# Recurrence: three block levels in one TensorE visit, differences of inputs and r0 on VectorE

## The chip, the cores and the metric

The kernel runs on one core of a Trainium2 chip. The metric is the device time of one execution in microseconds. The median of three runs before the change is 2112.96 us (2112.58 to 2113.19).

## The reference

A trunk of two decoder layers on 1024 tokens of width 1024, all in float32. Layer 0 mixes tokens with a gated linear recurrence (8 heads of 128), layer 1 with sliding-window attention; each is followed by a gated FFN of width 2816 with a causal convolution of width 3. Only the recurrence is touched here:

```python
def hgrn2_chunkwise(q, k, v, log_f):
    """S_t = diag(f_t) S_{t-1} + k_t v_t^T ; o_t = S_t^T q_t, evaluated chunk by chunk."""
    ...
def hgrn2_mixer(h, w_in, lower_bound, g_norm_w, w_out):
    q, f, i, g = jnp.split(h @ w_in, 4, axis=-1)
    fg = lb + (1.0 - lb) * jax.nn.sigmoid(heads(f))
    o = hgrn2_chunkwise(jax.nn.silu(heads(q)), 1.0 - fg, heads(i), jnp.log(fg))
    o = o * lax.rsqrt(jnp.mean(jnp.square(o), -1, keepdims=True) + RMS_EPS)
    o = o * g_norm_w.astype(jnp.float32) * jax.nn.silu(heads(g))
    return o.reshape(B, S, D).astype(h.dtype) @ w_out
```

## The kernel before, in words

**Number form.** Large products run in fp32r. Each operand is split into a high part and a low part; a product is three matmuls (`mm3`, L200 to L202: high-high, high-low, low-high). ScalarE casts the high part, VectorE subtracts it from the source to give the low part (`low_part`, L175).

**First stage (the first 47 us).** The input `x` comes in eight blocks of 128 tokens. `turn_keep` turns a block on TensorE (L210), ScalarE copies it twice (L959 the high part into `T`, L960 the exact values into `XS`), VectorE makes the low part (L175). `ig_block` multiplies a block with the first head's `i` and `g` weights: per `kc` one matmul of the high part with both weight parts (L846, 512 columns) and one of the low part with the high weights (L847, 256 columns). `lower_bounds` (L1004 to L1018) computes the gates' lower bounds with small instructions on VectorE and an exponential on ScalarE (L1013). Meanwhile GpSimd makes differences of quarters of `x` in place (`sums_of`, L902, 12 of them, 512 columns each) for the fast products that follow; `split_sum` splits them into high (ScalarE, L912) and low (VectorE, L913) parts in `HL` and in `T`, and L924 makes one more sum.

**Second stage.** The products of `f` and `q` of head 0 (96 matmuls), then 14 units (`q`+`f`, or `i`+`g`, of heads 1 to 7). A unit is seven products of half size after Strassen and Winograd (`product(u, p)`, 12 matmuls each), whose weight sums are made by VectorE (L1359, L1595) and split into `WR` (L1350 high, L175 low).

**Recurrence.** `recur` works one head in seven levels: at level i, blocks of 2^i tokens are joined in pairs. `update(i)` (L1171, L1173, L1176 on VectorE) multiplies the decays of a pair into `qp` and `kp`. The scores of level i take `qp` and `kp` as they stand before `update(i)`; where TensorE comes later, `stash(i)` keeps a copy of what the update will overwrite (two copies on ScalarE). Within 32 tokens the scores go to `Ab` (`scores`), above that to `A` (`blocks`): both use matmuls on 32 of the array's columns (`tile_position`), the one at output partition o on column group o/32. TensorE comes to a head in six visits, each squeezed between the 512-column matmuls of the units: (A) levels 8 and 4, column sums of `r0`, `r1`, `r2`; (B) levels 32 and 16; (C) eight transposes of `kp` and level 64; then the products of `kd` with `V`, of `A` with `V` and of `qp` with the state `St`. `r0 = qs * kp` is made by GpSimd (L1182), `r1` by VectorE (L1187).

**What sets the order.** In this part of the program the order on each engine is the order in which the code is laid out. The object `od` (class `Order`) keeps three clocks with estimated costs: `t` for TensorE, `v` for VectorE, `a` for ScalarE. Chains are generators that yield how long they want to wait on TensorE's clock; `od.tick()` after each matmul resumes those that are due. VectorE's small jobs (low parts "lo", weight sums "sum", parts of `x` "x") wait in the list `jobs` and are laid by `lay` when VectorE's clock leaves room, by `need` when a product asks for them, by `breathe` between a head's steps when they are pressing. Before the change, a loop (`while not prepared`) lays the whole preparation of the first unit ahead of the first head's recurrence.

Of the kernel before, what the change touches and what calls it, by code (L numbers as in the profile page):

```python
# [113 lines left out]
def trunk(ctx: ExitStack, tc: tile.TileContext, a: dict, out: bass.AP):  # L114
# [594 lines left out]
    with tc.tile_pool(name="t", bufs=1, reuse_waits="tile") as raws, hgrn_pool as hp:  # L709
# [34 lines left out]
        def group(key):  # L744
            return key[1] if key and key[0] in ("sum", "lo") else key[0] if key else None
# [9 lines left out]
        def first_ready(due=lambda key: True):  # L755
            seen = set()
# [19 lines left out]
        def pressing(key):  # L776
            if not key or key[0] not in ("sum", "lo"):
                return False
            if key[0] == "lo" and key[2] == 4:
                return True  # L780
            p = key[2] if key[0] == "lo" else {1: 5, 2: 6, 3: 7, 4: 4}[key[2]]
            return place_of[key[1], p] <= now[0] + (2 if key[0] == "lo" else 3)
# [54 lines left out]
        def ig_block(us, tp, ahead=None):  # L837
# [4 lines left out]
            for tb in () if ahead else (2 * tp, 2 * tp + 1):  # L842
                ps, ts = psmm(), slice(tb * P, (tb + 1) * P)
                for kc in range(KC):
                    w = us[kc // 4]
                    nc.tensor.matmul(ps, T[:, 0, kc, ts], w[:, :, kc % 4, :], start=kc == 0, stop=False)  # L846
                    nc.tensor.matmul(ps[:, :256], T[:, 1, kc, ts], w[:, 0, kc % 4, :], start=False, stop=kc == KC - 1)  # L847
                    od.t += 0.347
# [50 lines left out]
        def sums_of(t, eng):  # L899
            a11, a12, a21, a22 = [quarter(b, i) for b in (t, t + 4) for i in range(2)]  # L900
            for dst, x0, x1 in ((a11, a21, a11), (a21, a22, a21), (a22, a11, a22)):
                eng.tensor_tensor(dst, x0, x1, op=sub)  # L902
# [13 lines left out]
        def build_sums(go, summed):  # L916
            for t in range(4):
                while t not in summed:
                    yield 0.2
                for which in (7, 6):  # L920
                    split_sum(t, which)
                    yield 0.6
                a12, a22 = quarter(t, 1), quarter(t + 4, 1)
                job(od.t, 0.69, lambda a12=a12, a22=a22: nc.vector.scalar_tensor_tensor(  # L924
                    a12, a22, -1.0, a12, op0=ALU.mult, op1=sub), ("rows", t))
            left = {5: [0, 1, 2, 3], 3: [0, 1, 2, 3]}
            while left[5] or left[3]:
                which = 5 if left[5] and (go or not left[3]) else 3
                while which == 5 and not go:
                    yield 0.2  # L930
                t = left[which].pop(0)
                while which == 3 and ("rows", t) not in done_jobs:
                    yield 0.2
                split_sum(t, which)
                yield 0.6

        with tc.tile_pool(name="ep", bufs=1, reuse_waits="tile") as ep:
# [15 lines left out]
            def turn_keep(tb):  # L953
# [7 lines left out]
                low_part(T[:, 1, :, ts], by_k(XS[:, tb, :]), T[:, 0, :, ts], None)  # L961
# [13 lines left out]
            if True:  # L975
# [28 lines left out]
                def lower_bounds():  # L1004
# [6 lines left out]
                    for r in range(2):  # L1011
                        nc.vector.tensor_tensor(le[:, r, :], par[:, 8 * r:8 * r + 8], lm, op=ALU.subtract)
                    nc.scalar.activation(le, le, AF.Exp)  # L1013
# [19 lines left out]
                def first_split(g, names):  # L1033
                    w0[g] = [hp.tile([P, S], F32R, name=n).rearrange("p (k c) -> p k c", k=KC) for n in names]
                    hi, lo, raw = w0[g][0], w0[g][1], raws0[g].rearrange("p (k c) -> p k c", k=KC)
                    nc.scalar.copy(hi, raw)
                    low_part(lo, raw, hi, None)

                od.fill = lay
                go, summed = [], []  # L1040
                for t in range(2):
                    sums_of(t, nc.gpsimd)
                firsts = [od.spawn(build_sums(go, summed))]
                for tp, after in ((2, 2), (1, 6)):
# [4 lines left out]
                    if after == 2:  # L1049
                        summed.extend((0, 1))  # L1050
                for t in range(2, 4):
                    sums_of(t, nc.gpsimd)
# [5 lines left out]
                summed.extend((2, 3))  # L1058
# [1083 lines left out]
```

## Time and profile before

| | |
|---|---|
| median of three runs | 2112.96 us |
| the profiled execution | 2110.27 us |
| its span, first to last instruction | 2108.5 us |
| mean granted TensorE clock | 0.998 |
| busy: TensorE / VectorE / ScalarE / GpSimd | 2087.6 / 1803.3 / 972.5 / 317.3 us |
| first stage, to the first product of `f` | 0 to 46.76 us |
| units and recurrence | to about 470 us |

How to read it: PE is TensorE's matmuls, PEld its weight loads, DVE VectorE, ACT ScalarE, POOL GpSimd. A matmul in fp32 leaves two records in the trace, so 16 such matmuls show as x32; the start of one record to the start of the next tells the pace, since the durations overlap. `<-` in brackets names what ended the engine's idle time. "L847" is line 847 of the kernel printed above.

### The profile page before, as it was taken

How to read it: one execution, taken by the hardware profiler on the slowest of the kernel's cores; microseconds unless marked ns; L12 is line 12 of the kernel's file. 1: busy time of each engine (PE TensorE's matmuls, PEld its weight loads, DVE VectorE, ACT ScalarE, POOL GpSimd, SP SyncE). 2: the span in 40 equal slices, each digit the busy share in tenths (PEclk: the TensorE clock that was granted, in tenths of full speed). 3: DMA queues.
4: the chain of work that ended last, by engine and by line, in shares of the span. 5: the costliest groups of instructions: out<-in, count | busy, mean ns of one | idle time of the engine just before them, and what ended most of it. 6: DMA issues, size and time to landing. Idle time of an engine off the chain costs nothing.

```text
span 2108.5 us, 31814 instructions
## 1 busy us (share of the span) xinstructions
PE 2087.6 (99%) x12305; PEld 1741.4 (83%) x12305; DVE 1803.3 (86%) x2434; ACT 972.5 (46%) x1576; POOL 317.3 (15%) x323
## 2 busy tenths in 40 slices
PE   8999999999999999999999999999999999999998
PEld 7788888888888888888888888888888888888887
DVE  6978887779999998987977668979999999978986
ACT  5655555542444444444433367733544344444430
POOL 5011111201021122100001123312121122000002
PEclk9999999999999999999999999999999999999999
DMA  4111111324245577638754511052355577559662
GB/s 157 36 46 51 53 51 55 98 85 169 86 149 181 170 158 166 145 113 302 250 190 160 150 36 46 14 169 82 99 166 177 158 169 160 130 158 329 220 213 93
DMA packets 241303, 286.82 MB, mean 136 GB/s; under 512 B 30136, under 2 KB 160112, under 8 KB 241152
## 3 DMA queue, kind: packets, MB, share of 16 engines
q1 hardware_dynamic: 221600, 235.11, 34.6%
q0 software_dynamic: 19264, 49.54, 10.9%
q8 instruction: 97, 1.59, 0.3%
q14 instruction: 54, 0.44, 0.1%
q10 hardware_dynamic: 288, 0.14, 0.0%
HBM read 241.72 MB, written 89.15 MB: 157 GB/s over the span
## 4 chain that ended last, share of the span: by engine, by line
PE 94%; DVE 4%; issue 1%; ACT 1%; DMA 0%; SPq 0%; DVEq 0%; ACTq 0%
PE psmm L200 18%; PE psmm L202 18%; PE psmm L201 18%; PE psax L200 10%; PE psax L201 10%; PE psax L202 10%; PE psax L206 4%; PE psmm L206 1%; PE psmm L210 1%; PE psax L1916 1%; PE psax L210 1%; PE psmm L1743 1%; DVE T L175 0%; DVE r L1187 0%; DVE Y L261 0%
## 5 line engine op out<-in xcount | busy, mean ns | idle before, releaser
L507 DVE SCALAR_TENSOR_TENSOR Y<-Y,cwt 128x1023 f32<-128x1023 f32 (+1 forms) x176 | 225.0, 1281 | 46.1 <-ACT Y L505 44.7
L227 ACT CAST HL<-rx 128x1024 fp32r<-128x1024 f32 (+1 forms) x151 | 151.0, 1006 | 166.2 <-DMA rx<-in_ffn_w_in_dram 39.6
L200 PE MATMUL psmm<-T,HL 128*128 128x512 f32 x512 | 200.6, 392 | 0.0
L202 PE MATMUL psmm<-T,HL 128*128 128x512 f32 x512 | 199.3, 389 | 0.0
L201 PE MATMUL psmm<-T,HL 128*128 128x512 f32 x512 | 199.3, 389 | 0.0
L175 DVE TENSOR_TENSOR HL<-rx,HL 128x1024 fp32r<-128x1024 f32 (+1 forms) x151 | 176.4, 1175 | 17.9 <-ACT HL L227 17.6
L249 POOL TENSOR_TENSOR rs<-rs,nhalf 128x1 f32<-128x1 f32 x32 | 45.3, 1416 | 716.7 <-DVE rs L248 716.7
L505 ACT ACTIVATE Y<-Y,cwt 128x1024 f32<-128x1024 f32 x88 | 108.9, 1238 | 84.7 <-DVE Y L494 79.8
L200 PE MATMUL psax<-T,HL 128*128 128x512 f32 x352 | 137.3, 390 | 0.0
L202 PE MATMUL psax<-T,HL 128*128 128x512 f32 x352 | 137.0, 389 | 0.0
L201 PE MATMUL psax<-T,HL 128*128 128x512 f32 x352 | 136.9, 389 | 0.0
L549 POOL COPY warm<-Y 128x1 f32<-128x1 f32 x64 | 63.4, 990 | 356.3 <-DVE Y L488 349.3
L202 PEld LDWEIGHTS psmm<-T,HL 128*128 128x128 f32 x512 | 96.1, 188 | 20.1
L201 PEld LDWEIGHTS psmm<-T,HL 128*128 128x128 f32 x512 | 96.2, 188 | 19.5
L200 PEld LDWEIGHTS psmm<-T,HL 128*128 128x128 f32 x512 | 96.1, 188 | 19.6
L227 ACT CAST HT<-rx 128x1024 fp32r<-128x1024 f32 (+1 forms) x37 | 35.6, 962 | 133.5 <-DVE rx L462 66.7
L200 PE MATMUL psmm<-T,WR 128*128 128x512 f32 x224 | 90.3, 403 | 0.5 <-DVE GT L1464 0.5
L202 PE MATMUL psmm<-T,WR 128*128 128x512 f32 x224 | 87.4, 390 | 0.0
L201 PE MATMUL psmm<-T,WR 128*128 128x512 f32 x224 | 87.3, 390 | 0.0
L227 ACT CAST HL<-Y 128x1024 fp32r<-128x1024 f32 (+1 forms) x32 | 28.6, 893 | 118.2 <-DVE Y L462 41.2
L202 PEld LDWEIGHTS psax<-T,HL 128*128 128x128 f32 x352 | 66.1, 188 | 13.8
L200 PEld LDWEIGHTS psax<-T,HL 128*128 128x128 f32 x352 | 66.1, 188 | 13.6
(444 smaller groups left out, 6017.1 us busy)
## 6 DMA issues: line engine op xcount, KB each, us to landing
rx<-in_ffn_w_in_dram SPq DMA_DIRECT2D x136, 256.0 KB, 3.8
rx<-gd SPq DMA_DIRECT2D x118, 256.0 KB, 3.7
bsd<-in_ffn_w_out_dram POOLq DMA_DIRECT2D x36, 768.0 KB, 7.2
gd<-Y SPq DMA_DIRECT2D x44, 512.0 KB, 2.6
raw<-in_hgrn_w_in_dram SPq DMA_DIRECT2D x30, 512.0 KB, 5.1
rx<-in_ffn_w_out_dram SPq DMA_DIRECT2D x54, 256.0 KB, 4.5
R<-bsd SPq DMA_DIRECT2D x44, 256.0 KB, 5.1
Y<-in_ffn_w_in_dram SPq DMA_DIRECT2D x40, 256.0 KB, 3.8
```

The costliest lines, as they stand in the source:

```text
L175: make = lambda e: e.tensor_tensor(lo, src, hi.bitcast(F32), op=ALU.subtract)
L200: nc.tensor.matmul(ps, st(0), mv(0), start=start, stop=False, skip_group_check=more)
L201: nc.tensor.matmul(ps, st(0), mv(1), start=False, stop=False, skip_group_check=more)
L202: nc.tensor.matmul(ps, st(1), mv(0), start=False, stop=stop, skip_group_check=more)
L206: nc.tensor.matmul(ps, lhsT, rhs, start=start, stop=stop, **kw)
L210: nc.tensor.transpose(ps, src, ident)
L227: nc.scalar.copy(hi, src)
L249: nc.gpsimd.tensor_tensor(rs, rs, nhalf, op=ALU.pow)
L505: nc.scalar.activation(c, u, AF.Identity, bias=cwt[:, l, 3, ci:ci + 1], scale=cwt[:, l, 2, ci:ci + 1])
L507: nc.vector.scalar_tensor_tensor(c[:, sh:], u[:, :S - sh], cwt[:, l, 2 - sh, ci:ci + 1], c[:, sh:], op0=ALU.mult, op1=ALU.add)
L549: with tc.issue_after(nc.gpsimd.tensor_copy(tick, Y[:, 2 * (fc % 2) + (p == 4), :1]).ins):
L1743: nc.tensor.matmul(ps, T[:, x, kc, tb * P:(tb + 1) * P], us[kc][:, w, :], start=start and kc == 0, stop=False)
```

## The change

1. **Blocks of x.** In `ig_block` the eight matmuls with the high part come first, then the eight with the low part. The low part becomes a job that is laid at the latest between the two (`need(("T", tb))`). In `lower_bounds`, 2.6 us of the planner's time lie ahead of the exponential.
2. **Differences.** The 12 differences of quarters move from GpSimd to VectorE, as jobs "xs"; `build_sums` becomes one chain for each pair of blocks.
3. **First unit.** The loop that laid its preparation in one piece is gone; it is laid beside the first products and the first head.
4. **Planner.** Among the jobs that are ready, the one with the earliest `deadline` is laid, the place of the product that needs it.
5. **r0** moves from GpSimd to VectorE.
6. **Levels 16, 32 and 64.** They go in one visit (B) after `update(5)`: level 64 straight from `kp` and `qp`, level 32 from a `stash(5)` that replaces `stash(6)`. Level 64 is cut into 32 matmuls of 32 columns on four column groups, where there were 16 of 64 columns on two. The transposes of `kp` stay as visit (C). Level 64 is copied to `A` in two pieces.

```diff
@@ planner
+        def deadline(key):
+            if not key or key[0] not in ("sum", "lo") or key[0] == "lo" and key[2] == 4:
+                return -2 if key and key[0] == "T" else -1
+            return place_of[key[1], key[2] if key[0] == "lo" else {1: 5, 2: 6, 3: 7, 4: 4}[key[2]]]
@@ first_ready
                 if ready <= max(od.t, od.v) and due(key):
-                    return i
+                    found.append((deadline(key), i))
+            return min(found)[1] if found else None
@@ ig_block
                 for kc in range(KC):
-                    w = us[kc // 4]
-                    nc.tensor.matmul(ps, T[:, 0, kc, ts], w[:, :, kc % 4, :], start=kc == 0, stop=False)
-                    nc.tensor.matmul(ps[:, :256], T[:, 1, kc, ts], w[:, 0, kc % 4, :], start=False, stop=kc == KC - 1)
-                    od.t += 0.347
+                    nc.tensor.matmul(ps, T[:, 0, kc, ts], us[kc // 4][:, :, kc % 4, :], start=kc == 0, stop=False)
+                    od.t += 0.23
+                    od.tick()
+                if ("T", tb) in pending:
+                    need(("T", tb))
+                for kc in range(KC):
+                    nc.tensor.matmul(ps[:, :256], T[:, 1, kc, ts], us[kc // 4][:, 0, kc % 4, :], start=False, stop=kc == KC - 1)
+                    od.t += 0.117
                     od.tick()
@@ sums_of
-        def sums_of(t, eng):
+        def sums_of(t):
             a11, a12, a21, a22 = [quarter(b, i) for b in (t, t + 4) for i in range(2)]
-            for dst, x0, x1 in ((a11, a21, a11), (a21, a22, a21), (a22, a11, a22)):
-                eng.tensor_tensor(dst, x0, x1, op=sub)
+            for n, (dst, x0, x1) in enumerate(((a11, a21, a11), (a21, a22, a21), (a22, a11, a22))):
+                job(kept[t + 4], 0.61, lambda dst=dst, x0=x0, x1=x1: tt(dst, x0, x1, op=sub), ("xs", t, n))
@@ turn_keep
-                low_part(T[:, 1, :, ts], by_k(XS[:, tb, :]), T[:, 0, :, ts], None)
+                kept[tb] = od.act(2.05)
+                job(od.a, 1.23, lambda: low_part(T[:, 1, :, ts], by_k(XS[:, tb, :]), T[:, 0, :, ts], None), ("T", tb))
+                pending.add(("T", tb))
@@ lower_bounds
+                    yield 2.6
                     nc.scalar.activation(le, le, AF.Exp)
@@ blocks
                 m = 1 << i
+                if m == 2 * BL:
+                    for c in range(NB):
+                        for u in range(2):
+                            for b in range(2):
+                                o, t = m * u + BL * b, c * P + m + BL * u
+                                mm32(pv[o:o + BL, c, m:m + BL], K[:, c * P + BL * b:c * P + BL * (b + 1)], Q[:, t:t + BL],
+                                     cost=0.015, tile_position=(0, o))
+
+                    def put():
+                        for u in range(2):
+                            nc.scalar.copy(A[:m, :, m + BL * u:m + BL * (u + 1)], pv[m * u:m * (u + 1), :, m:m + BL])
+                            od.act(0.4)
+                    return put
@@ recur
-            nc.gpsimd.tensor_tensor(r0, qs, kp, op=ALU.mult)
+            nc.vector.tensor_tensor(r0, qs, kp, op=ALU.mult)
...
+                if j == 0:
+                    next_early = stash(5, hp.tile([P, S], F32, name="St"))
+            yield max(od.a - od.t - 0.2, 0.0)
+            yield from update(5)
+            yield od.behind(0.6, 0.5)
             pv = chunks(psax())
-            high, low = blocks(5, pv, kp, qp), scores(4, pv[:, :, :16], early, early)
-            yield from update(5)
+            last_put = blocks(6, pv, kp, qp)
+            high, low = blocks(5, pv, next_early, next_early), scores(4, pv[:, :, :16], early, early)
+            yield from update(6)
             low()
-            yield od.behind(-0.6, 0.0)
-            early = stash(6, hp.tile([P, S], F32, name="kd"))
-            yield max(od.a - od.t - 0.2, 0.0)
-            yield from update(6)
-            wait = od.behind(0.6, 2.1)
             high()
+            last_put()
...
-            put = blocks(6, chunks(psax()), early, early)
             kd = hp.tile([P, S], F32, name="kd")
             nc.scalar.copy(kd, ps)
-            put()
@@ product
-            if (u, p) in prep:
-                drive(lambda: prep[u, p][1] is None)
+            drive(lambda: (u, p) in casted)
@@ before the units
-            while not prepared:
-                for t in firsts:
-                    if t[1] is not None:
-                        od.step(t)
-                if jobs:
-                    lay_job()
             task = od.spawn(all_heads())
```

Three places in the orders that come out. TensorE at the first full block of `x` (block 4), where `psmm` is the block's accumulator and `psax` takes the transposes of the blocks to come. Before, and then after:

```order
L877 MATMUL psmm<-HL,T 128x256 x8
L846 MATMUL psmm<-HL,T 128x512
L847 MATMUL psmm<-HL,T 128x256
L846 MATMUL psmm<-HL,T 128x512
L847 MATMUL psmm<-HL,T 128x256
```

```order
L884 MATMUL psmm<-HL,T 128x256 x8
L848 MATMUL psmm<-HL,T 128x512 x8
L854 MATMUL psmm<-HL,T 128x256 x3
L210 MATMUL psax<-ident,XS 128x128 x8
L854 MATMUL psmm<-HL,T 128x256 x5
```

The alternation of high and low is gone; the transposes of blocks 2 and 6 now stand among the low passes.

VectorE at the same place: `par`, `lm`, `le`, `lbt` belong to the lower bounds, `T<-XS` is the low part of a block (first block 4, then block 5). Before, and then after:

```order
L175 TENSOR_TENSOR T<-XS,T 128x8x128
L1008 COPY par<-psmm 128x17
L1009 TENSOR_SCALAR par<-par 128x1
L1010 TENSOR_TENSOR lm<-par 128x8
L1012 TENSOR_TENSOR le<-par,lm 128x8 x2
L1015 TENSOR_TENSOR lm<-le 128x8
L1016 RECIPROCAL lm<-lm 128x8
L1017 TENSOR_TENSOR lbt<-le,lm 128x8
L1018 TENSOR_SCALAR lbt<-lbt 128x8
L175 TENSOR_TENSOR T<-XS,T 128x8x128
```

```order
L1023 TENSOR_TENSOR le<-par,lm 128x8 x2
L1027 TENSOR_TENSOR lm<-le 128x8
L1028 RECIPROCAL lm<-lm 128x8
L1029 TENSOR_TENSOR lbt<-le,lm 128x8
L1030 TENSOR_SCALAR lbt<-lbt 128x8
L175 TENSOR_TENSOR T<-XS,T 128x8x128
L909 TENSOR_TENSOR XS<-XS 128x512
L175 TENSOR_TENSOR T<-XS,T 128x8x128
```

The low part of block 4 now stands behind the lower bounds, and the differences (L909) stand among the low parts.

TensorE at the third visit (C) of head 0, between matmuls of the units, where `ident,kp` are the transposes and `psax<-kd` is level 64. Before, and then after:

```order
L201 MATMUL psmm<-T,WR 128x512
L202 MATMUL psmm<-T,WR 128x512
L210 MATMUL psax<-ident,kp 128x128 x8
L206 MATMUL psax<-kd 32x64 x16
L200 MATMUL psmm<-T,WR 128x512
```

```order
L201 MATMUL psmm<-HL,WR 128x512
L202 MATMUL psmm<-HL,WR 128x512
L210 MATMUL psax<-ident,kp 128x128 x8
L200 MATMUL psmm<-HL,WR 128x512
L201 MATMUL psmm<-HL,WR 128x512
```

Level 64 has left this visit; it stands in the one before (B) as 32 matmuls of 32x32 ahead of the other two levels.

More of the change, by code (lines that the diff above doesn't have):

```diff
@@ L744, in group @@
         def group(key):
-            return key[1] if key and key[0] in ("sum", "lo") else key[0] if key else None
+            if not key or key[0] not in ("sum", "lo"):
+                return key[0] if key else None
+            return key if key[0] == "lo" and key[2] > 3 else key[1]
+        def deadline(key):
+            if not key or key[0] not in ("sum", "lo") or key[0] == "lo" and key[2] == 4:
+                return -2 if key and key[0] == "T" else -1
+            return place_of[key[1], key[2] if key[0] == "lo" else {1: 5, 2: 6, 3: 7, 4: 4}[key[2]]]
         def lay_job(i=0):
@@ L776, in pressing @@
         def pressing(key):
[L777 to L782, printed above, removed]
+            return bool(key) and key[0] in ("sum", "lo") and deadline(key) <= now[0] + (2 if key[0] == "lo" else 3)
         def breathe():
@@ L914, in split_sum, with build_sums @@
                 ("x", which, t))
[L916 to L933, printed above, removed]
+        kept, pending = {}, set()
+        def build_sums(t, go):
+            while t + 4 not in kept:
+                yield 0.2
+            sums_of(t)
+            while ("xs", t, 2) not in done_jobs:
+                yield 0.2
+            yield max(laid_at["xs", t, 2] - od.t, 0.0)
+            for which in (7, 6):
                 split_sum(t, which)
                 yield 0.6
+            a12, a22 = quarter(t, 1), quarter(t + 4, 1)
+            job(od.t, 0.69, lambda: nc.vector.scalar_tensor_tensor(a12, a22, -1.0, a12, op0=ALU.mult, op1=sub), ("rows", t))
+            while ("rows", t) not in done_jobs or not go:
+                yield 0.2
+            yield max(laid_at["rows", t] - od.t, 0.0)
+            split_sum(t, 3)
+            while len(go) < 2:
+                yield 0.2
+            yield 0.3
+            split_sum(t, 5)
         with tc.tile_pool(name="ep", bufs=1, reuse_waits="tile") as ep:
@@ L1036, in first_split @@
                     nc.scalar.copy(hi, raw)
+                    od.act(1.07)
                     low_part(lo, raw, hi, None)
+                    od.v = max(od.v, od.a)
+                    od.vec(1.23)
                 od.fill = lay
[L1040 to L1043, printed above, removed]
+                go = []
+                for t in range(4):
+                    od.spawn(build_sums(t, go))
                 for tp, after in ((2, 2), (1, 6)):
@@ L1048, in trunk @@
                     soon_all(1)
[L1049 to L1052, printed above, removed]
                 first_split("f", ("qp", "tot"))
@@ L1057, in trunk @@
                 nc.vector.tensor_copy(msk, mf)
-                summed.extend((2, 3))
+                go.append(0)
         def conv_load(l, k):
@@ L1239, in recur @@
             od.act(1.64, od.v)
-            yield wait
+            yield od.behind(0.6, 0.5)
             off = level[1]
@@ L1584, in drive @@
             raise ValueError("the order never comes to its end")
-        prepared, WR, ring_pool = [], [], ExitStack()
+        casted, WR, ring_pool = set(), [], ExitStack()
         def first_unit():
-            while ("x", 5, 3) not in done_jobs or ("x", 3, 3) not in done_jobs:
+            while not all(("x", which, t) in done_jobs for which in (3, 5, 6, 7) for t in range(4)):
                 yield 0.2
```

13 lines of the change are left out of this document (6 added, 7 removed).

## Prediction

> **What bounds the kernel now.** I read the page's busy shares first, then the waits of TensorE (PE), then the timeline of PE where it waits, and of VectorE (DVE), ScalarE (ACT) and GpSimd (POOL) at the same places.
>
> ```profile
> PE 2087.6 (99%) x12305; PEld 1741.4 (83%) x12305; DVE 1803.3 (86%) x2434; ACT 972.5 (46%) x1576; POOL 317.3 (15%) x323
> ```
>
> ```profile
> PE psmm L847 <- DVE T L175: 4.9, 2, 3.2
> PE psmm L200 <- DVE GT L1464: 1.6, 2, 1.1
> PE psmm L846 <- ACT T L959: 1.5, 1, 1.5
> ```
>
> PE is the bound: it is busy for 99% of the span. Time can be won only by taking work from its queue or by ending one of its waits. Nearly all waits lie in the first 85 us, where the first head's inputs are made:
>
> ```profile
> 13.30:17.60 4.30, 4.30 (x38) 4.14 (x36) 1.02 (x2) 2.58 (x4) 0.94 (x1) 1.00 1.07 394
> 17.60:46.76 29.16, 22.78 (x131) 19.33 (x129) 23.71 (x30) 16.27 (x29) 21.64 (x14) 0.95 0.21 66
> 46.76:84.35 37.59, 36.01 (x158) 29.16 (x157) 33.93 (x57) 24.38 (x45) 2.71 (x2) 1.00 0.21 58
> 43.70:47.00 3.30, 3.30 (x12) 2.82 (x11) 3.30 (x4) 0.00 (x0) 3.00 (x4) 0.50 0.02 3
> ```
>
> (The second number is the stretch's length; then busy time of PE, PEld, DVE, ACT and POOL, the granted clock, DMA.) In the second stretch, the six blocks of `ig_block`, PE is idle for 6.4 of 29.16 us, and for 3.3 us after its longest wait the granted clock is 0.50.
>
> **Part 1: the input blocks.** PE's rows there:
>
> ```profile
> 25.52 1.04 PE L210 MATMUL psax<-ident,XS 128*128 128x128 f32 x8
> 26.31 0.48 PE L846 MATMUL psmm<-HL,T 128*128 128x512 f32 x1
> ...
> 34.13 0.39 PE L846 MATMUL psmm<-HL,T 128*128 128x512 f32 x1
> ...
> 39.08 0.39 PE L846 MATMUL psmm<-HL,T 128*128 128x512 f32 x1
> 42.69 0.39 PE L847 MATMUL psmm<-HL,T 128*128 128x256 f32 x1 [3.21 <-DVE T L175]
> ...
> 46.76 0.54 PE L200 MATMUL psmm<-T,qp 128*128 128x512 f32 x1
> ```
>
> Undisturbed, 14 pairs (L846 with L847) go from 34.13 to 39.08: 0.354 us each. Eight transposes take 26.31 - 25.52 = 0.79. The stretch 17.60 to 46.76 holds 48 pairs and four groups of transposes: 48 x 0.354 + 4 x 0.79 = 20.1 us of work, so 9.0 us are lost to waits and to the slow clock. The waits are for the high part of a block (ACT) and for its low part (DVE). Why they come late is on these engines:
>
> ```profile
> 15.57 1.02 ACT L960 COPY XS<-psax 128x1024 f32<-128x1024 f32 x1
> 20.43 0.22 ACT L1013 ACTIVATE le<-le 128x16 f32<-128x16 f32 x1 [3.85 <-DVE le L1012]
> ...
> 22.07 0.99 ACT L959 CAST T<-psax 128x1024 fp32r<-128x1024 f32 x1
> ```
>
> ```profile
> 18.04 0.98 DVE L1010 TENSOR_TENSOR lm<-par 128x8 f32<-128x8 f32 x1
> 19.06 1.34 DVE L1012 TENSOR_TENSOR le<-par,lm 128x8 f32<-128x8 f32 x2
> ...
> 24.01 1.23 DVE L175 TENSOR_TENSOR T<-XS,T 128x1024 fp32r<-128x1024 f32 x1 [1.61 <-ACT XS L960]
> ...
> 36.96 3.47 DVE L913 SCALAR_TENSOR_TENSOR HL<-XS,HL 128x512 fp32r<-128x512 f32 x2
> 40.35 2.28 DVE L175 TENSOR_TENSOR T<-XS,T 128x1024 fp32r<-128x1024 f32 x1
> ...
> 44.56 2.29 DVE L175 TENSOR_TENSOR tot<-raw,qp 128x1024 fp32r<-128x1024 f32 x1
> ...
> 52.04 1.29 DVE L913 SCALAR_TENSOR_TENSOR HL<-XS,HL 128x512 fp32r<-128x512 f32 x2
> ```
>
> ```profile
> L924 DVE SCALAR_TENSOR_TENSOR XS<-XS 128x512 f32<-128x512 f32 x4 | 3.7, 932 | 0.0
> ...
> L1017 DVE TENSOR_TENSOR lbt<-le,lm 128x8 f32<-128x8 f32 x1 | 0.2, 168 | 0.0
> ```
>
> ```profile
> L902 POOL TENSOR_TENSOR XS<-XS x12: 1278/1664/2337, 16.7 to 44.2; 128x512 f32<-128x512 f32 x12
> ```
>
> Two things delay them. ACT's exponential (L1013) sits 3.85 us in its queue, waiting for DVE, with block 5's copy (22.07) behind it. And while POOL makes a difference (L902, median 1664 ns), a DVE instruction is stretched: the same pair of L913 takes 3.47 us with POOL at work and 1.29 without, the low part 2.28 and 1.23, an instruction on 8 columns 0.98 (L1010) and 0.17 (L1017). The change ends both: the exponential is laid behind block 5's copies, POOL has no differences. And the low passes now stand behind all eight high passes of a block, 1.8 us later.
>
> It brings one new wait: DVE now does the lower bounds ahead of block 4's low part. By the rows: ACT ends block 4's copies at 16.6, takes block 5's two from 16.8 (0.9 each), the exponential at 18.7 to 18.9; DVE's four small instructions behind it I put at 0.8, the low part at 1.23: ready at 21.0. PE needs it at 17.60 + 8 x 0.227 = 19.4: 1.6 us of waiting. Walking the later blocks through the new order with the same durations, each high and low part is there first, the last (block 7) within 0.1 us. So the first product of `f` starts at 17.60 + 20.1 + 1.6 = 39.3 and not at 46.76: **7.5 us won**. Bounds: 9.0 (no wait left) and 2.5 (the three waits of 6.4 us stay, the new one takes the place of none, and only the slow clock goes). I take 7.5, since the walk finds no second wait.
>
> **Part 2: VectorE up to the first visit.** The 12 differences and `r0` move to DVE. Prices, undisturbed:
>
> ```profile
> 67.87 2.49 DVE L175 TENSOR_TENSOR WR<-raw,WR 128x512 fp32r<-128x512 f32 x4
> 70.39 1.23 DVE L1183 TENSOR_TENSOR qp<-qs,fg 128x1024 f32<-128x1024 f32 x1
> ```
>
> ```profile
> L1187 DVE TENSOR_TENSOR r<-kp,qp x8: 678/2740/2786, 71.7 to 414.8; 128x512 f32<-128x512 f32 x8
> ```
>
> 512 columns in a row cost 0.61 (2.49 for four, the last one's end included), 1024 cost 1.14 to 1.23. Added: 12 x 0.61 + 1.2 + two jobs drawn ahead (1.2) = 9.7 us. Gone is the stretching in the rows shown: L1010 0.8, L1012 0.9, L913 2.2, the low part 1.05, `tot` 1.05, the four of L924 1.0 (932 against 680 ns), L1187 behind POOL's `r0` 2.05 (2740 against 678 ns): 9.0 us. DVE was idle for 4.30 - 1.02 + 29.16 - 23.71 + 37.59 - 33.93 = 12.4 us from 13.3 to 84.35; in the walk about 8 stay (par, the exponential, V and GV from ACT, the first WR). So `kp` of level 2, ready at 84.3 now, comes at about 84.3 - 9.0 + 9.7 - 4.4 = 80.6. PE now runs 177 matmuls, not 156, ahead of that visit:
>
> ```profile
> 91.65 0.39 PE L200 MATMUL psmm<-T,WR 128*128 128x512 f32 x1
> ...
> 95.50 0.39 PE L202 MATMUL psmm<-T,WR 128*128 128x512 f32 x1
> 95.82 0.66 PE L206 MATMUL psax<-qp,kp 128*32 128x32 f32 x29
> ...
> 96.35 0.73 PE L206 MATMUL psax<-kd 128*32 128x16 f32 x62
> 97.00 0.50 PE L200 MATMUL psmm<-T,WR 128*128 128x512 f32 x1
> ```
>
> 17 intervals from 91.65 to 95.50: 0.2265 us each. PE arrives at 39.3 + 177 x 0.2265 = 79.4 and waits 1.2 us. Now 37.59 - 156 x 0.2265 = 2.3 us are lost before that visit, so **1.1** is won. Bounds: 2.3, and minus 2.5 (DVE 3.6 us later than I sum). In later heads `r0` leaves DVE 0.9 us freer each (2.06 of stretch against 1.14); PE does not wait for it there, so it counts nothing.
>
> **Part 3: the visits of the recurrence.** What a visit costs now:
>
> ```profile
> 84.35 0.70 PE L206 MATMUL psax<-qp,kp 128*32 128x16 f32 x62 [1.19 <-DVE kp L1173]
> ...
> 84.92 0.70 PE L206 MATMUL psax<-A 128*32 128x16 f32 x60
> ```
>
> ```profile
> 103.94 1.03 PE L210 MATMUL psax<-ident,kp 128*128 128x128 f32 x8
> 104.91 1.09 PE L206 MATMUL psax<-kd 128*32 128x64 f32 x32
> 105.93 0.50 PE L200 MATMUL psmm<-T,WR 128*128 128x512 f32 x1
> ```
>
> Level 64 (`blocks(6)`, 16 products of 64 columns, two records each) stands behind the transposes: 105.93 - 103.94 = 1.99 us together, of which the transposes alone are 0.79. Taking it out saves 1.20. It comes back in the visit at 95.82 as 32 products of 32 columns on four column groups, 64 records. Their price is not in the trace. From below: 64 records of 16 columns on four groups take 84.92 - 84.35 = 0.57, 9 ns each; 32 records of 32 columns on two groups take 96.35 - 95.82 = 0.53, 16.6 ns each, 33 per group, which over four groups is 8.3 ns. From above: 64 x 16.6 = 1.06, if four groups run no faster than two. I take 0.57, as 16 columns on four groups already pass at 9 ns a record. So 0.63 a head, **5.0 us** over eight (1.1 to 5.4). The number of visits does not fall: the transposes keep theirs. Three times (heads 1, 2 and 7) the old order has tile work straight behind transposes, which cost 104.91 - 103.94 - 0.79 = 0.18 at the join; the new order has none: **0.5**. ScalarE copies level 64 in two pieces, one instruction more a head; at 46% busy it is hidden, and `put` is waited for only by the product with V, two steps later. Were ACT late there, that product would be late next.
>
> [...]
>
> **Part 4: the rest.** The planner's new deadlines reorder DVE's jobs for all 14 units. The largest of PE's other waits, L200 on GT, is 1.6 us in two places; I leave it and the smaller ones as they are. Bounds: 1.6 less, and 8 more if every second unit gets one like the longest, 1.1. From the FFN on, the order is the same. The work of PE is shifted, not changed.
>
> Sum: 7.5 + 1.1 + 5.0 + 0.5 = 14.1. The profiled execution took 2110.27 (2.7 below the median of the runs), so 2096.2 there; from the median of 2112.96, 2098.9.
>
> **The rivals.**
> - VectorE becomes the bound of the first 85 us: it has 9.7 us more to do and my idle time of 8 us is a guess. If it is 5 us later than summed, PE waits 5 us more at the first visit or for the products' weights ahead of it: 2104. For it: DVE is busy 33.93 of 37.59 us there; against it: the stretching is measured.
> - Four column groups run like two: part 3 gives 1.1 and not 5.0, 2102.8. Against it: 9 ns a record.
> - Better: the waits of part 4 shrink, since deadlines now order the low parts, 1.6, and the two new ones, 1.6 and 1.2, do not come: 2094.5.
> - Slower: the deadlines keep a unit's low parts behind other jobs, so a product waits for them. At 1.4 us for each of 14 units, 19.6, less the 14.1: 2118.5. It decides from 1.0 us a unit. Against it: DVE's waits on PE's side are two of 1.6 us in all now, and DVE gets 0.9 us a head freer.
>
> **How the numbers follow.** My forecast 0.60 (2096 to 2102), VectorE 0.17, better 0.11, column groups 0.07, slower 0.05. A measurement of this kernel cannot tell 0.2%, 4.2 us, from no change: 2108.7 to 2117.2. The first four end below 2108.7; allowing for two mishaps together, faster 0.88, same 0.08, slower 0.04. The better case reaches lower than its 2094.5 by the 1.2 of part 2; the slower ones and VectorE's by as much upward. Leaving out one in ten at each end: 2092.5 to 2107.5.
>
> **What would show it.** Right: PE's first L200 near 39 us; one wait of about 1.6 us near 19 us and none of 3; no half clock near 44; the merged visit 1.8 us long and the transposes' 0.8; POOL without TENSOR_TENSOR there and L1212, the old L1187, at 0.7. Wrong: PE waiting for kp or WR between 57 and 85 us, or for low parts in later units, or the tile records at 16 ns.

## The result, and the profile after

The changed kernel takes 2101.59 us (median of 4 runs, 2097.58 to 2102.22); the kernel before, run beside it, 2113.07 (2112.58 to 2113.97). The ratio is 0.9941, 95% interval 0.9924 to 0.9958: 11.5 us faster where 14.1 were forecast, 2.7 above the predicted 2098.9 and inside the range. The profiled execution took 2101.76 (span 2099.9) against 2110.27 before: 8.5 less. It is near the top of its kernel's runs, that of before below the middle of its own (2109.72 to 2114.01 over 26 runs), so the traces show less than the medians.

The page's busy row, then the largest of TensorE's waits (total, times, longest):

```profile
PE 2080.2 (99%) x12561; PEld 1736.0 (83%) x12561; DVE 1795.8 (86%) x2454; ACT 972.9 (46%) x1584; POOL 270.8 (13%) x303
```

```profile
PE psax L206 <- issue: 2.0, 1, 2.0
PE psmm L200 <- issue: 2.0, 1, 2.0
PE psmm L210 <- ACT Y L413: 1.7, 1, 1.7
PE psmm L854 <- DVE T L175: 1.3, 1, 1.3
```

The waits of the input blocks, 4.9 us for low parts and 1.5 for a high part before, are down to one of 1.3 for a low part. New are two of 2.0 that wait for "issue": nothing that the profile shows holds the instruction back. The stretches of the first part, with the borders of before (4.3 us ahead of block 4, block 4's start, first product of `f`, first visit), and the half clock:

```profile
12.60:16.90 4.30, 4.30 (x37) 4.14 (x37) 0.69 (x6) 3.34 (x5) 0.00 (x0) 1.00 1.08 393
16.90:38.73 21.83, 20.52 (x130) 18.16 (x129) 17.38 (x31) 15.69 (x30) 0.00 (x0) 1.00 0.31 98
38.73:79.35 40.62, 40.31 (x180) 33.06 (x178) 38.32 (x65) 24.98 (x47) 0.00 (x0) 1.00 0.18 52
420.50:424.00 3.50, 3.50 (x28) 2.10 (x28) 1.14 (x3) 1.21 (x3) 0.95 (x1) 0.51 0.31 119
```

29.16 us have become 21.83. ScalarE no longer waits with block 5's copy behind it: that copy starts at 16.14, where it started at 22.07, and the exponential (L1025) follows without idle time:

```profile
16.14 1.02 ACT L968 CAST T<-psax 128x1024 fp32r<-128x1024 f32 x1 [0.25 <-PE psax L210]
...
17.96 0.23 ACT L1025 ACTIVATE le<-le 128x16 f32<-128x16 f32 x1
```

The slow stretch of the clock that lay at 43.7 has gone, but one as long stands at 420.6, straight behind one of the new waits. TensorE's rows at the two new waits, each with the idle time and its releaser in brackets:

```profile
172.94 0.30 PE L1078 MATMUL psax<-ident,cr 88*128 88x88 f32 x1
175.20 0.40 PE L200 MATMUL psmm<-T,WR 128*128 128x512 f32 x1 [1.97 <-issue]
...
417.70 0.71 PE L206 MATMUL psax<-A 128*32 128x16 f32 x61
420.45 0.18 PE L206 MATMUL psax<-A 128*32 128x16 f32 x1 [2.04 <-issue]
```

The first visit, head 0's common visit of levels 64, 32 and 16, and its transposes:

```profile
79.35 0.70 PE L206 MATMUL psax<-qp,kp 128*32 128x16 f32 x62 [0.31 <-DVE kp L1196]
...
92.55 0.39 PE L202 MATMUL psmm<-T,WR 128*128 128x512 f32 x1
92.87 0.73 PE L206 MATMUL psax<-qp,kp 128*32 128x32 f32 x62
93.41 0.20 PE L206 MATMUL psax<-St 128*32 128x32 f32 x1
...
94.57 0.50 PE L200 MATMUL psmm<-T,WR 128*128 128x512 f32 x1
...
97.41 1.03 PE L210 MATMUL psax<-ident,kp 128*128 128x128 f32 x8
98.20 0.48 PE L200 MATMUL psmm<-HL,WR 128*128 128x512 f32 x1
```

The 64 records of level 64 take 93.41 - 92.87 = 0.54 us. From the start of the last product ahead of it to the next one behind it, the common visit takes 94.57 - 92.55 = 2.02 (1.50 before, with two levels) and the third visit, counted in the same way, 1.02 (2.21 before). On VectorE, the group of `r1` (the old L1187, 2740 ns in the median before) and that of the differences:

```profile
L1212 DVE TENSOR_TENSOR r<-kp,qp 128x512 f32<-128x512 f32 x8 | 5.5, 689 | 0.2
L909 DVE TENSOR_TENSOR XS<-XS 128x512 f32<-128x512 f32 x12 | 8.2, 688 | 0.1
```

### The profile page after: what moved, and what is told of

The parts are those of the page before. It is cut to its first block, busy times and chain, and to the rows that moved or that the text cites. A ratio compares the mean times of both kernels' runs of the same rounds, so it can differ in the third digit from the quotient of the medians.

```text
span 2099.9 us, 32302 instructions
## 1 busy us (share of the span) xinstructions
PE 2080.2 (99%) x12561; PEld 1736.0 (83%) x12561; DVE 1795.8 (86%) x2454; ACT 972.9 (46%) x1584; POOL 270.8 (13%) x303
## 3 DMA queue, kind: packets, MB, share of 16 engines
q8 instruction: 99, 1.62, 0.3%
## 4 chain that ended last, share of the span: by engine, by line
PE 92%; DVE 5%; ACT 2%; issue 1%; DMA 0%; POOL 0%; SPq 0%; DVEq 0%; ACTq 0%; POOLq 0%
PE psmm L200 18%; PE psmm L202 18%; PE psmm L201 18%; PE psax L200 10%; PE psax L202 10%; PE psax L201 10%; PE psax L206 3%; PE psmm L206 1%; PE psmm L210 1%; PE psax L1931 1%; PE psax L210 1%; PE psmm L1758 1%; DVE T L175 0%; DVE Y L261 0%; DVE HL L920 0%
## 5 line engine op out<-in xcount | busy, mean ns | idle before, releaser
L200 PE MATMUL psmm<-T,HL 128*128 128x512 f32 x512 | 200.6, 392 | 0.0
L175 DVE TENSOR_TENSOR HL<-rx,HL 128x1024 fp32r<-128x1024 f32 (+1 forms) x151 | 176.5, 1176 | 16.3 <-ACT HL L227 15.9
L249 POOL TENSOR_TENSOR rs<-rs,nhalf 128x1 f32<-128x1 f32 x32 | 46.5, 1454 | 714.2 <-DVE rs L248 714.2
L200 PE MATMUL psax<-T,HL 128*128 128x512 f32 x352 | 137.3, 390 | 0.0
L200 PEld LDWEIGHTS psmm<-T,HL 128*128 128x128 f32 x512 | 96.2, 188 | 19.5
L200 PE MATMUL psmm<-T,WR 128*128 128x512 f32 x224 | 89.7, 400 | 2.0 <-issue 2.0
L175 DVE TENSOR_TENSOR WR<-raw,WR 128x512 fp32r<-128x512 f32 x98 | 64.9, 687 | 17.8 <-ACT WR L1374 17.6
L202 PEld LDWEIGHTS psax<-T,HL 128*128 128x128 f32 x352 | 66.1, 188 | 13.8
```

Source lines behind the costliest of these rows:

```text
L175: make = lambda e: e.tensor_tensor(lo, src, hi.bitcast(F32), op=ALU.subtract)
L200: nc.tensor.matmul(ps, st(0), mv(0), start=start, stop=False, skip_group_check=more)
L202: nc.tensor.matmul(ps, st(1), mv(0), start=False, stop=stop, skip_group_check=more)
L249: nc.gpsimd.tensor_tensor(rs, rs, nhalf, op=ALU.pow)
```

## The experiments

Three sets ran, each on one chip beside the kernel before: the changed kernel again with three edits (before: 2113.24), then four edits (2112.22), then four (2111.84). The kernel before differs by 1.4 us between the sets, so times of two sets are compared less sharply than their ratios. Single executions of one kernel differ by some 5 us (2097.58 to 2102.23, 2109.72 to 2114.01); in the traces a half clock of 3.41 us (1.7 us of work) stands behind some stalls and not behind others. So each kernel is read by its trace, and its time is the check.

**The base.**

> The changed kernel once more, unchanged, as the base of this set. Theory A (TensorE runs dry of instructions): the four stalls that the chain shows as issue (1.97 us at 175.20, 0.44 at 282.66, 2.04 at 420.45, 0.25 at 441.85) come back at the same instructions, since the piece borders are fixed by the program; the half clock of 3.4 us after the one at 420 may be there or not, 1.65 us. Theory B (chance of one execution, a transfer or a neighbour): the stalls lie elsewhere or are missing. Time 2101.6, or 2099.9 without the half clock.

2100.48 us (ratio to before 0.9942, interval 0.9929 to 0.9954; so written below too). Stalls: 1.98 at 175.37, 0.61 at 283.05, 2.30 at 421.07, at the same instructions as before; the one of 0.25 is missing, and no half clock came ahead of the program's end. The place is the program's, the size and the clock are the execution's.

**What "issue" is.** I counted TensorE's instructions (matmul records, weight loads and its waits for semaphores) in order of their starts. Ahead of the first instruction that each of the four stalls of the first profile holds back stand 3265, 5825, 8641 and 9153 others: 193 + 256 x 12, x 22, x 33 and x 35. The trace also has a queue named "instruction", with packets of 16 KB:

```profile
q8 instruction: 99, 1.62, 0.3%
```

99 packets for 25,316 instructions (97 for 24,807 before): 256 each in the mean, so I take them for TensorE's list. To move the borders I lengthened the warm-up; all other instructions kept their order.

```
-                for n in (9, 3):
+                for n in (7, 3):          # 128 columns each, as before
...
+                        for i in range(30):   # 18 in the second kernel
+                            o = i % 4 * BL
+                            nc.tensor.matmul(idle[o:o + BL, :16], still[:, :BL], still[:, :16], tile_position=(0, o), ...)
```

> The same with eighteen small products, so that the list is moved by 16 products, 64 instructions. Theory A: stalls stand at other visits, about 2.3 us at head 1's first visit (near 124), 1.5 at head 3's second visit (near 235), 2.0 at head 5's first visit (near 323) and 0.9 at head 6's second visit (near 387), and none at 175 and 420: 6.5 us for 4.7, so 2103.4 with a half clock somewhere and 2101.7 without. Theory B: as before the shift, 2101.6.

2101.91 us (0.9947, 0.9934 to 0.9959). The stalls have left 175, 282, 421 and stand at 125.97 (1.62), 236.57 (2.22), 325.58 (1.31) and 390.55 (0.41), the four named places, in other sizes than the 2.3, 1.5, 2.0 and 0.9 that I had named:

```profile
125.97 0.50 PE L200 MATMUL psmm<-HL,WR 128*128 128x512 f32 x1 [1.62 <-issue]
...
236.57 0.26 PE L206 MATMUL psax<-kd 128*32 128x16 f32 x9 [2.22 <-issue]
```

> Only TensorE's warm-up ahead of the first block is changed: two of its products of 128 columns less, thirty of 16 columns on four column groups more, so that everything behind stands 28 products, 112 instructions (a record and its weight load each, two of them a product), later in TensorE's list. Theory A: the list is fetched in pieces of 256 instructions, all four stalls lie at a border (193 + 256 k in the profile's count), and a stall comes where a whole piece is run in less time than a fetch takes, about 1.1 to 2.2 us to its start and 2.4 more. With the borders 112 earlier no border falls so: the four stalls (4.7 us) and the half clock behind one of them (1.65) go, and at most 0.2 us comes elsewhere (near 189 us): 2101.6 - 6.3 = 2095.3. Theory B (the stalls belong to the visits, their operands or their order): they stay where they are, 2101.6.

2103.03 us (0.9949, 0.9936 to 0.9963), where 2095.3 was expected. The old places are free, so the stalls do follow the borders; but others came, 1.82 at 83.36, 3.26 at 129.38 and 0.44 at 391.94, 5.5 us in all, each again at 193 + 256 k of this kernel's count:

```profile
129.38 0.42 PE L206 MATMUL psax<-St,one 128*32 128x256 f32 x4 [3.26 <-issue]
```

My forecast of the sizes failed. Sixteen instructions ahead of the border before the first of them, TensorE stood at its wait for `kp` (0.3 us); that this delayed the packet is not shown. The packet ahead of the second starts at 126.96, 2.3 us after the border before is run; why it starts there is not shown either.

**Block 4's low part first.**

```
                     nc.scalar.activation(warm, nhalf, AF.Sigmoid)
+                    t0 = od.t
+                    need(("T", 4))
+                    od.t = t0
                     nc.vector.tensor_tensor(lm, le[:, 0, :], le[:, 1, :], op=ALU.add)
```

> VectorE makes block 4's low part ahead of the lower bounds' last four instructions and not behind them; nothing else moves. Theory A (my sum): the wait of 1.31 us at 20.22 is the new wait that I forecast, caused by that order; it goes, the first product of f starts at 37.4 instead of 38.7, VectorE's idle time of 2.9 us there takes the low part up, and kp of the first visit comes earlier too: 2101.6 - 1.3 = 2100.3. Rival: the wait is ScalarE's (its copy of block 4 ends at 15.9) and stays, or the gain comes back as a wait of 1.6 us for kp at the first visit: 2101.6.

2098.72 us (0.9936, 0.9924 to 0.9949), 1.8 under the base; the two intervals overlap, so the trace decides. From block 4 to the first product of `f` it takes 20.25 us, and TensorE does not wait:

```profile
16.50:36.75 20.25, 20.25 (x130) 18.23 (x129) 16.40 (x31) 15.76 (x31) 0.00 (x0) 1.00 0.33 104
```

The 1.31 was the order of two of VectorE's jobs, as forecast, and was not given back: the first visit waits 0.16.

**The order of high and low passes.**

```
                     nc.tensor.matmul(ps, T[:, 0, kc, ts], ...)
-                    od.tick()
-                if ("T", tb) in pending:
-                    need(("T", tb))
-                for kc in range(KC):
+                    if kc == 0 and ("T", tb) in pending:
+                        need(("T", tb))
                     nc.tensor.matmul(ps[:, :256], T[:, 1, kc, ts], ...)
```

> The six input blocks take their high and low passes in turns again, as before the change; the differences stay on VectorE and the lower bounds stay as changed. Theory A: the new order of the passes is one of the causes of the 8 us won there, worth up to 1.8 us at every block whose low part is late. Block 4's low part comes at 20.2, PE needs it at 17.1 and not at 18.9: a wait of 3.1 for 1.3; a second and third of up to 1 us at later blocks. First product of f at 40.5 to 42.5 for 38.7, time 2102 to 2104. Rival: with VectorE and ScalarE early enough the order of the passes counts only at block 4, 1.8 us, or nothing.

2108.05 us (0.9979, 0.9970 to 0.9988), more than the 2102 to 2104 that I had expected. The stretch to the first product of `f` is 25.74 us, 3.9 longer:

```profile
17.73:43.47 25.74, 22.58 (x131) 19.70 (x129) 20.15 (x38) 17.37 (x34) 0.00 (x0) 0.93 0.25 76
```

The wait for block 4's low part is 2.92 (3.1 forecast), one more is 0.24, and a half clock follows, 1.7. The profiled executions differ by 9.3 in all; the rest is block 4's start 0.6 later, a wait of 1.74 for WR at 75.77 in place of 0.3 for `kp`, 1.6 more of stalls and a second half clock, 1.7.

**The differences on GpSimd.** In a first version the low parts of blocks 4 to 7 stood behind the differences and were made of differenced blocks, which changes part of the result and lets them wait for GpSimd.

> The twelve differences of the input's quarters go back to GpSimd, all else as changed. Theory A: GpSimd's work stretches VectorE's again (2.28 us for a low part of 1.23, 3.47 for two of L920's kind that take 1.29), so low parts come later and PE waits for them: the first product of f 1 to 4 us later, 40 to 43; VectorE has 7.3 us less of its own and about 7 of stretching more, so kp of the first visit stays near its time and the wait there shrinks as the rest grows. Time 2101.5 to 2104.5. Rival: the passes' order and the bounds' place did all of it, and the time stays at 2100.5.

It took 2110.82 us; TensorE waited 3.51, 2.57 and 0.72 for low parts. The version that answers the question makes each low part first:

```
-                job(kept[t + 4], 0.61, lambda ...: tt(dst, x0, x1, op=sub), ("xs", t, n))
+                nc.gpsimd.tensor_tensor(dst, x0, x1, op=sub)
...
+            while ("T", t + 4) not in done_jobs:
+                yield 0.2
             sums_of(t)
```

> The twelve differences go back to GpSimd, each block's low part made ahead of them, all else as changed. Theory A: GpSimd's work stretches VectorE's beside it (a low part 2.28 us for 1.23), so low parts come later and PE waits for them: from block 4's start to the first product of f 23 to 26 us for 21.8, time 2101.5 to 2104.5 by 1 to 4 us more there. Rival: VectorE has 7.3 us less of its own to do, which makes up for the stretching, and the stretch stays at 21.8 and the time at 2100.5.

2104.28 us (0.9964, 0.9950 to 0.9978). The stretch is 23.2 us, at the lower end of theory A, with VectorE's low parts stretched as before the change (first stretched row, then an undisturbed one):

```profile
21.02 2.08 DVE L175 TENSOR_TENSOR T<-XS,T 128x1024 fp32r<-128x1024 f32 x1
...
34.59 1.23 DVE L175 TENSOR_TENSOR T<-XS,T 128x1024 fp32r<-128x1024 f32 x1 [0.67 <-ACT XS L969]
```

So the differences are worth 1.4 us here and 1.1 behind it (waits of 0.54 and 0.83 for `tot` and `og` for one of 0.28). The profiled executions differ by 4.9; most of the rest is 1.0 more of stalls and a half clock, 1.7, less a wait of 0.9 in the FFN. The order of the passes, with its half clock, is worth 3.9. The place of the exponential was not tried alone; in all kernels with the new place TensorE has no wait for a high part of a block.

**`r0` on GpSimd.**

```
-            nc.vector.tensor_tensor(r0, qs, kp, op=ALU.mult)
+            nc.gpsimd.tensor_tensor(r0, qs, kp, op=ALU.mult)
```

> Each head's first product r0 goes back to GpSimd, with the order of all other instructions as changed. Theory A (my prediction's bookkeeping): beside it VectorE's product r1 takes 2.7 us and not 0.7, against 1.14 of its own saved, so VectorE is 0.9 us later; PE feels it at the first visit, where it already waits 0.3 (1.2 then), and at no later head: 2100.5 + 0.9 = 2101.4. Rival: VectorE's lead is short at every head, so PE waits at each: up to 7 us, 2107.

2106.01 us (0.9974, 0.9962 to 0.9986), 5.5 above the base, but not by the rival's road: VectorE is stretched, the first visit waits 0.66 for 0.29, and no other visit waits for `kp`. In the first head it is the low part ahead of `r1` that runs beside GpSimd's `r0`, and not `r1`, which takes 0.7 to 2.8 us in the eight heads, 2.1 in the mean:

```profile
64.96 2.53 DVE L175 TENSOR_TENSOR WR<-raw,WR 128x512 fp32r<-128x512 f32 x1 [0.28 <-ACT WR L1374]
67.41 0.68 DVE L1212 TENSOR_TENSOR r<-kp,qp 128x512 f32<-128x512 f32 x1
```

The rest is stalls at borders, five for three, 6.5 us for 4.9, and two half clocks (at 176.5 and 425.7) for none: 0.4 + 1.6 + 3.4 = 5.4 of the 5.8 by which the profiled executions differ. Why the same borders stalled longer is not shown.

**Level 64: visit or column groups?** Three kernels: all 64 records on two groups, in the common visit; the old 16 products of 64 columns there (the branch `if m == 2 * BL` taken out); and the kernel before with that branch put in, level 64 staying in the third visit. The first one's edit:

```
-                                o, t = m * u + BL * b, c * P + m + BL * u
-                                mm32(pv[o:o + BL, c, m:m + BL], ...
+                                o, t = BL * b, c * P + m + BL * u
+                                mm32(pv[o:o + BL, c, m + BL * u:m + BL * (u + 1)], ...
```

> Level 64 keeps its 64 records of 32 columns and its place in the second visit, but all of them go to two column groups (rows 0 to 63) and not to four; the number and order of instructions stay, so the borders of the instruction pieces stay too. Theory A (the price in my prediction): the groups work side by side, a record costs 9 ns on four groups and 16.6 ns on two, so the second visit grows from 1.8 to about 2.3 us, 0.49 a head, 3.9 us over eight. Rival: a record costs 9 ns wherever it is put (the issue of the instructions is the limit), and nothing changes. Time: 2100.5 + 3.9 = 2104.4 by A, 2100.5 by the rival, each with 1.7 us for a half clock that may come or not.

2103.76 us (0.9964, 0.9950 to 0.9978). The common visit takes 2.50 us, 0.48 more; that is 3.9 over eight heads, and the time is 3.3 above the base, 4.6 by the ratios. Level 64's rows there end at 94.03 from 93.05, 0.98 us for 64 records: 15 ns each where four groups give 8.4.

```profile
93.05 1.17 PE L206 MATMUL psax<-qp,kp 128*32 128x32 f32 x61
94.03 0.22 PE L206 MATMUL psax<-St 128*32 128x32 f32 x1
```

> The kernel before with one part of the change: level 64 stays in the third visit behind the transposes, but is made of 32 products of 32 columns on four column groups. Theory A: the gain of the visits comes from the splitting, 1.20 - 0.57 = 0.63 a head, so the third visit falls from 2.2 to about 1.6 us and the time by 5.0: 2113.2 - 5.0 = 2108.2. Rival: the gain comes from the common visit (no join between transposes and tile work), and here at most 0.1 a head is won: 2112.4. Half clocks and stalls at instruction borders, which lie elsewhere with 32 records a head more, may add up to 4 either way; so the third visit's own length decides.

2117.3 us (1.0021, 1.0012 to 1.0030). The third visit, from the start of the last product ahead of it (108.10) to that of the next behind it (109.99), takes 1.89 us: 0.32 less than before, half of what I had expected, and far more than the rival's 0.1.

```profile
108.10 0.39 PE L202 MATMUL psmm<-T,WR 128*128 128x512 f32 x1
108.34 1.03 PE L210 MATMUL psax<-ident,kp 128*128 128x128 f32 x8
109.30 0.76 PE L206 MATMUL psax<-kd 128*32 128x32 f32 x64
109.99 0.50 PE L200 MATMUL psmm<-T,WR 128*128 128x512 f32 x1
```

The time hides it: in the profiled execution block 4 starts 1.7 us later, a wait of 5.15 at 485.29 (0.54 before, at the same L200) goes back to VectorE waiting for the load of `Y`'s input, a stall of 2.03 comes, and the half clocks ahead of the end are 17.1 us long in all for 3.4. Why most of this kernel's ten executions, 2113.4 to 2118.3, are longer than those of before is not shown beyond this one.

> Level 64 stays in the common second visit but is made as before the change, of 16 products of 64 columns on two column groups, 32 records and not 64. Theory A (the columns that pass a group set the price): 32 records x 33 ns = 1.06 us as for the 64 records on two groups, so the second visit takes 2.5 us and not 2.0, and third visits stay at 1.0. Rival: the number of records sets it, and the visit falls below 2.0. With the second run of this set (two groups, third visit's splitting) it says what of the 0.67 us a head is the common visit's and what the four groups'. The time holds stalls at other borders (64 instructions a head less) and is not used.

2095.82 us (0.9924, 0.9910 to 0.9938). The common visit takes 94.60 - 92.22 = 2.38 us, 0.36 more than with four groups and 0.12 less than forecast.

```profile
92.22 0.39 PE L202 MATMUL psmm<-T,WR 128*128 128x512 f32 x1
92.54 1.02 PE L206 MATMUL psax<-qp,kp 128*32 128x64 f32 x29
93.35 0.22 PE L206 MATMUL psax<-St 128*32 128x32 f32 x1
...
94.60 0.51 PE L200 MATMUL psmm<-T,WR 128*128 128x512 f32 x1
```

Yet this kernel looks faster than the changed one: its four runs (2095.28 to 2096.42) all lie below the nine of that one (2097.58 to 2102.23). They come from another set, whose kernel before was up to 1.4 us faster, and the intervals of the ratios overlap, so the trace has to say why. It has 64 instructions a head less, its borders fall elsewhere, and in its trace there is no stall at a border and no half clock ahead of the end.

```profile
79.02:457.69 378.67, 377.45 (x4005) 317.31 (x4005) 305.04 (x542) 215.55 (x466) 35.45 (x40) 1.00 0.20 60
```

From the first visit to the end of the recurrence it needs 378.67 us where the changed kernel needs 383.57 (79.35 to 462.92), though its visits are 2.9 longer.

**The better version.** Block 4's low part first, and 42 small products in the warm-up.

> Block 4's low part ahead of the lower bounds, and forty-two small products in the warm-up (two wide ones less), which moves TensorE's list by 160 instructions. Theory A (instruction pieces): stalls at the borders 193 + 256 k of the new numbering only. From the times of the profile, with a fetch starting 1.1 us after the list is read to a border (50 instructions ahead of the running one) or up to 3.5 where transfers fill the queues, and usable 2.4 later, three remain, 0.65 near 96, 0.4 near 140 and 0.8 near 337, 1.8 us for 4.9, and fewer half clocks: 2098.7 - 3.1 = 2095.6, with 1.7 less where a half clock is missing. [...] Rival: stalls of some 5 us come wherever the borders fall, 2098.7.

2095.56 us (0.9926, 0.9914 to 0.9939): the time is as forecast, the reason isn't. The profiled execution, at 2098.0 the slowest of the five, has stalls of 2.18, 0.68, 1.15 and 0.75 at borders, 4.8 us and not 1.8, and a half clock. What it has less than the kernel with block 4's low part first alone is one half clock and 1.2 us of a later wait (0.44 for 1.68 at the transposes of layer 0's FFN); its stalls are 0.7 longer. That moving the borders by 160 helped is not shown; the two ratios' intervals overlap.

## Why the prediction was right, and where it was off

The sum against the profiled executions, term by term:

| term | forecast | measured |
|---|---|---|
| block 4's start, no term (17.60, now 16.90) | 0 | -0.7 |
| part 1, block 4 to the first product of `f` | -7.5 | -7.3 (29.16 to 21.83) |
| part 2, lost ahead of the first visit | -1.1 | -1.7 (2.26 to 0.53) |
| part 3, visits | -5.0 | -5.4 (8 x 0.67) |
| part 3, joins at heads 1, 2 and 7 | -0.5 | -0.65 |
| part 4, the other waits and the clock | 0 | +7.0 |
| sum | -14.1 | -8.8; the traces differ by -8.5 |

- **Part 1** came as walked: one wait, 1.31 us at 20.22 for a forecast 1.6 at 19.4, none of 3, no half clock. The experiments confirm the order of the passes (3.9 with the clock), the differences (1.4, and 1.1 behind it) and the new wait's cause. The exponential's share is argued from the traces only: block 5's copy starts at 16.14 and not at 22.07, and the wait of 1.49 for a high part is gone.
- **Part 2**: the first visit at 79.35 for 79.4 + 1.2, with 0.31 of wait. `kp` came at 79.35 for a forecast 80.6; 0.7 of that is block 4's earlier start. The walk to it was wrong in two terms that cancelled. From 4.3 us ahead of block 4 to the first visit, VectorE's work fell by 2.3 us (0.69 + 17.38 + 38.32 for 1.02 + 23.71 + 33.93), where my sum had 9.7 - 9.0 = 0.7 more: it left out stretched rows, L1015 (1.07 for 0.17) and three of L824 (0.79 for 0.42). And VectorE's idle time stayed at 10.4, not at the 8 us that I had left in. The rival "VectorE becomes the bound" did not happen: 0.31 and 0.66 are all that TensorE waits for `kp`.
- **Part 3**: 64 records took 0.54 us (0.57 forecast), 8.4 ns each; the rival "like two" (2102.8) is ruled out. The merged visit was forecast at 1.8 us; from its first tile record it takes 94.57 - 92.87 = 1.70. Both prices of the sum held: the third visit lost 1.19 (1.20 forecast) and the common one grew by 0.52 (0.57). What the sum does not say is which of the two steps the 0.67 comes from, and there my expectations were wrong. The visits as pairs (second and third): 1.50 + 2.21 before; 1.50 + 1.89 with four groups in the old place; 2.38 + 1.02 in the common visit with the old 16 products; 2.02 + 1.02 with both. Each step alone is worth 0.31 or 0.32 us, together 0.67, where I had expected 0.63 for the splitting and, from 1.20 - 1.06, 0.14 for the common visit. By the rows, the old products take 93.35 - 92.54 = 0.81 in the common visit and not 1.06, and the 64 records 109.99 - 109.30 = 0.69 behind the transposes and not 0.57, both up to the start of the next row.
- **Part 4 is the step that failed**: "I leave it and the smaller ones as they are", 0 with bounds of -1.6 and +8. It is +7.0: stalls at borders of the instruction list +4.7 (1.97, 0.44, 2.04, 0.25), the half clock behind one of them +1.65, waits behind the recurrence (0.84, 0.56 and 1.67 for 0.31, 0.54 and 0.13) +2.1, less the old waits on the way, 2.2 gone and 0.7 new. It lay inside its bounds, but by a mechanism that I had not named: the bound was argued with low parts, and no product of a later unit waits for one. The rival of late low parts is ruled out.
- The wait of 1.67 at the FFN's first transposes (0.13 before) came as 0.4 to 1.7 in all kernels with the change but one, that with the differences on GpSimd. In the first profile a GpSimd instruction (L249) took 2.05 us and not 1.45 there; but five kernels in which it took 1.45 wait 0.8 to 1.1, so the cause stays open.

By the traces the sum promised 5.3 us too much: part 4 took 7.0 away, and parts 2 and 3 and block 4's start gave 1.9 more than forecast. Block 4's start is chance: it lies between 16.3 and 17.7 in the kernels with this change. That the medians come within 2.7 us of the forecast is in part luck: the profiled execution of before is 2.8 below its median, that of the changed kernel is at its own, and no trace shows what fills these 2.8.

## What to carry to other kernels

Where an engine runs hundreds of very short instructions in a row, look at its instruction queue as well: count the instructions of a packet (here 256 in the mean), and compare the time in which that many are run (3.2 to 4.4 us at the four stalls of the first profile, the stalls included) with the time from the packet's start to the stall's end (2.36 to 2.43 us there). A visit made denser in records can give its gain back there; fewer and wider products (here 16 of 64 columns for 32 of 32) may be the faster form though each visit is longer (2.38 us for 2.02, and 378.67 for 383.57 us from the first visit to the end of the recurrence). And when two causes are bundled, try each alone: a sum can be right and still not say what each is worth.

## What the runs showed of the hardware

In the 13 profiles with the change or a part of it there are 41 waits over 0.1 us at exactly 193 + 256 k of TensorE's count (as above, with the waits for semaphores), the three kernels with a moved list included. All 40 waits put down to "issue" are among them (one is put down to ACT), and the kernel before has none. Each ends 2.2 to 2.9 us, median 2.4, after a 16 KB packet of the instruction queue starts; in the first profile the packets start at 172.77, 280.30, 418.05 and 439.43, 2.43, 2.36, 2.40 and 2.42 us ahead of the four stalls' ends. In that profile, from 480 us on, the packet mostly starts when TensorE runs 10 to 43 instructions ahead of the border before, 31 in the median, so nearly 290 ahead of the next border (the 50 instructions and 1.1 us of the last expectation were estimates of mine), and no wait for "issue" stands there. Ahead of the 41 stalls the 256 instructions pass in 1.1 to 3.8 us, 2.1 in the median, the stall itself left out. A fast piece alone does not stall: in the first profile two pieces pass in 1.42 and 1.53 us without a stall (ending at 220.19 and 373.53), and their packets had started 1.2 us ahead of the border before, 2.65 and 2.80 us ahead of the need. Some packets start late: for the stall at 175.20 at 172.77, 1.95 us after the border before is run and three instructions ahead of the stalled one, with

```profile
q1 hardware_dynamic: 2050, 1.03, 44.5%
q0 software_dynamic: 208, 0.57, 18.7%
```

on the queues from 169 to 177. That these queues are what delays the packet is my reading; no run tried it.

Of the 21 stalls of 1.8 us or more, 12 were followed by a granted clock of 0.5, for 3.41 us or once for 6.83, the other 9 by none. The stall of 2.04 at 420.45 has a half clock behind it from 420.57 to 423.99, 1.7 us of work; the same one in the second execution, 2.30 at 421.07, has none (1.00 from 400 to 440), so it costs nearly 4 us there and 2.3 here. In the first profile and in that of before, the changes of the granted clock lie whole multiples of 3.413 us apart: 122, 1 and 491 of them (full clock from 4.15, half from 420.57, full from 423.99, half from 2096.52), and before 11, 1 and 604 (6.12, 43.66, 47.08, 2105.31). What decides whether a stall is followed by a half clock is not shown: no run tried it.
